# Expert weights two tiles to a transfer, in rows of 8 KB, with buffers given out in rows of two

## The chip, the cores and the metric

The program runs on one core of a Trainium2 chip. The metric is the device time of one execution in microseconds (us); the time before is the median of three runs. The profile is that of one execution of the same program.

## The reference

Two layers of a decoder work on 256 tokens of width 1024, all in float32. Each layer computes

```
h = rms(x); p = h @ W_in                       # q 8x64, k 2x64, v 2x64, u 512
x = x + W_o [ rms(window_attention(q,k,v)) ; rms(ssm(u)) ]
x = x + ffn(rms(x))
```

The feed-forward part of layer 0 is a dense SwiGLU, `(silu(h Wg) * (h Wu)) Wd` with an inner width of 3584. That of layer 1 is a mixture: a router picks two of eight such SwiGLU experts for every token, and the two results are added with softmax gates. The eight experts' weights are 352 MB of the 420 MB that the program reads from HBM (High Bandwidth Memory, the chip's main memory).

## The kernel before

**How the work is staged.** First the mixer of layer 0 (projection, attention, state-space model, output projection; until about 205 us), then the dense feed-forward part in 7 chunks of 512 inner columns (until about 450 us, with the mixer of layer 1 worked into its end), then the routing (480 to 494 us), then the experts (until 1407 us), then the output. The experts are sorted by how many tokens they got and taken in the order `TURNS = (0, 4, 1, 5, 2, 6, 3, 7)`: places 0 to 3 are heavy (room for 128 tokens), places 4 to 7 are light (room for 64). So a heavy expert and a light one alternate, each in 7 chunks.

**A chunk of an expert.** It takes 12 weight tiles, each of 128 partitions x 1024 float32 (512 KB, one DMA each, 4 KB to a partition): 4 of the gate matrix, 4 of the up matrix, 4 of the down matrix. To multiply float32 at one pass per column, `split` makes two fp32r tiles of a loaded tile `w`: ScalarE copies it, rounded, to `wh`, VectorE subtracts to get `wl = w - wh`. A heavy expert then has three matmuls for each of the two halves of a tile (`wh,xh`, `wl,xh`, `wh,xl`), 72 in a chunk. A light expert holds the high and the low half of its 64 tokens side by side in one operand (`lx`), has two matmuls per half tile, and folds the halves together afterwards (`join`). Of its 12 tiles one (`ENTIRE`) is not split but multiplied in plain float32. After gate and up come silu (ScalarE), a product on VectorE in `glu_up` or `light_up`, four transposes, a split of the result, and the down matmuls, which are written out one chunk late behind the next chunk's gate and up.

**Buffers.** All wide tiles come out of one pool `m` of `NM = 44` buffers of 4 KB a partition: `w`, `wh`, `wl`, the gathered tokens, the results. Narrower ones come out of a pool `h` of 8.

**What sets the order.** `Plan` records every operation, and `order` plays them through with modelled costs (`cost`, `lag`, `between`, `rate`) and priorities: the longest path to the end plus a hand-given number per stage (`BONUS`, 35 entries). The order in which operations start in this play is the order of the program, engine by engine; the play also counts free buffers, holds some back (`keep`, from `KR` and `LEAN`) and limits the split tiles alive. DMAs are all issued by SP (SyncE) in the order of the loads; a DMA whose buffer is not free yet waits on SP's queue, and everything behind it waits too. The loads of the first expert (place 0) name their address outright; later ones take the expert's number from a register, which is known once the routing is done.

**Names in the profile.** All operations are emitted by one line, L445 (`emit`), so rows are told apart by tile names: `w`, `wh`, `wl`, `xh`, `xl` (heavy tokens), `lx` (light tokens), `sg` (the product of gate and up), `ht`, `hth`, `htl` (its transposes), `yh`, `yl` (the result), `X` (the running x), `rw` (the router's weights).

The lines that load a tile and split it:

```python
    def load(self, src, whole=False):
        w = self.M("w")
        self.plan.keep = self.kr
        ...
        self.nc.sync.dma_start(w, src)
        ...
        return (w, None) if whole else self.split(w)
```

Of the kernel before, what the change touches and what calls it, by code (L numbers as in the profile page):

```python
# [26 lines left out]
ROOM = 64  # L27
# [40 lines left out]
class Buf:  # L68
    def __init__(self, plan, kind, shape, dtype, name):
        self.kind, self.shape, self.dtype, self.name = kind, shape, dtype, name  # L70
        self.real = None
        self.log = []
        self.users = 0
        self.live = False
        self.cols = int(np.prod(shape[1:]))
# [53 lines left out]

class Late:  # L130
# [19 lines left out]
class Plan:  # L150
    between, rate = 0.0027, 360e3

    def __init__(self):
        Plan.between, Plan.rate = 0.0027, 360e3
# [17 lines left out]
    def add(self, eng, method, a, k):  # L172
        i = len(self.ops)
        out = [x for x in (a[0], k.get("accum_out")) if isinstance(x, View)]
        src = [x for x in (*a[1:], *(v for n, v in k.items() if n != "accum_out")) if isinstance(x, View)]
# [35 lines left out]
    def cost(eng, method, a, k):  # L211
# [3 lines left out]
        if eng == "DMA":  # L215
            return int(np.prod(a[0].shape)) * 4 / Plan.rate + 0.01
# [7 lines left out]
        if eng == "ACT":  # L224
            return 0.05 + n * 0.000876 + (0.06 if any(isinstance(v, View) for v in k.values()) else 0)
        if eng == "POOL":
            return max(0.35, 0.05 + n * 0.0006)
        if method in ("tensor_scalar", "tensor_copy"):
# [6 lines left out]
    @staticmethod  # L235
    def lag(e, f):

        return 0.0 if e == f == "PE" else LAT[e] + (0.13 if f == "PE" and e != "DMA" else 0.0)

    def order(self, slots):  # L240
# [13 lines left out]
        for i, o in enumerate(ops):  # L254
            prio[i] += self.bonus.get(o["tag"], 0.0)
        free = dict(slots)
        engines = ["PE", "DVE", "ACT", "POOL", "DMA"]
# [48 lines left out]
        while done < n:  # L306
# [14 lines left out]
            while freed and freed[0][0] <= t:  # L321
                _, kd, name = heapq.heappop(freed)
                free[kd] += 1
                raw -= name == "w"
# [5 lines left out]
            while avail[e]:  # L330
# [7 lines left out]
                if (due or not o["turn"] or split < o["most"] and o["turn"] == turn) and all(  # L338
                        free[kd] - c >= (o["keep"] if kd == "m" and not due and (raw > 1 or not o["dma"]) else 0)
                        for kd, c in need.items()) and (due or not need or safe(x[1])):  # L340
# [35 lines left out]
            o = ops[i]  # L376
            for b in o["bufs"]:
# [33 lines left out]
            for b in o["bufs"]:  # L411
                users[id(b)] = users.get(id(b), 0) + 1
                if users[id(b)] == b.users and b.kind in free:
                    heapq.heappush(freed, (end, b.kind, b.name))
# [13 lines left out]
    def emit(self, nc, make, order):  # L428
# [11 lines left out]
        for i in order:  # L440
            o = self.ops[i]
            if o["method"] == "registers":
                o["a"][2](real(o["a"][1]))
                continue
            getattr(engines[o["eng"]], o["method"])(*map(real, o["a"]), **{n: real(v) for n, v in o["k"].items()})  # L445


class Kernel:
# [3 lines left out]
    BONUS = {'qkv1': -5, 'att0': 43, 'att0s': 29, 'prep0': 5, 'us1': -15, 'xt0': 8, 'ssm1y': -83, 'ssm0g': 60, 'u0': -47, 'wo01': 87, 'qkv0': 2, 'hn': -49, 'route': -33, 'wo011': 54, 'att1s': -26, 'prepo1': -82, 'moe': -5, 'route1': -2, 'att0v': 10, 'rs': -22, 'wo11': 8, 'ssm0': 3, 'route0': 42, 'ssm1': 5, 'wo010': -5, 'att1v': 40, 'xt1': 12, 'us0': 5, 'gates': 5, 'prep1': 15, 'ssm1g': 20, 'att1': 2, 'wo10': 2, 'wo110': -2, 'u1': -2}  # L452
# [3 lines left out]
    hold, spare = [], 0  # L456
# [8 lines left out]
    def __init__(self, tc, ctx, aps):  # L465
# [4 lines left out]
            ("k", 1, {}), ("m", self.NM, {}), ("h", self.NH, {}), ("s", 2, {}), ("ps", 8, {"space": PSUM}))}  # L470
# [5 lines left out]
    def make(self, b):  # L476
        return self.new(b.kind, b.shape, b.dtype, b.name)
# [34 lines left out]
    def load(self, src, whole=False):  # L512
        w = self.M("w")
# [4 lines left out]
        self.nc.sync.dma_start(w, src)  # L518
# [76 lines left out]
    def inv_rms_turned(self, x, n, name):  # L595
# [8 lines left out]
        return self.inv_root(bank[:, 0:2], n, name)  # L604

# [542 lines left out]
    def glu_up(self, src, of, blocks, rs):  # L1148
# [42 lines left out]
    def route(self, rs, gain):  # L1191
# [3 lines left out]
        rw = self.rw  # L1195
        tt(rw.rearrange("p (k e) -> p k e", k=8), self.rw.rearrange("p (k e) -> p k e", k=8),
# [117 lines left out]
    def gather(self, es, hn):  # L1314
# [13 lines left out]
        for b in range(2 * n):  # L1328
            bank = self.bank()
            for i in range(4 // n):  # L1330
                k = 4 // n * b + i
                for j, (x, t) in enumerate(src):
                    p = PP[:, m * t:m * t + m]
                    nc.tensor.matmul(bank[:, m * i:m * i + m], x[:, 128 * k:128 * k + 128], p if hn else p.bitcast(F32),
                                     start=j == 0, stop=j == len(src) - 1)
            for i in range(4 // n):
# [3 lines left out]
                g = self.mg[:, k:k + 1]  # L1340
# [389 lines left out]
```

## Time and profile before

| what | value |
|---|---|
| median of 3 runs | 1419.53 us (1416.21 to 1420.21) |
| the profiled execution | 1417.69 us, of it 1415.9 us from the first to the last instruction |
| TensorE busy, matmuls | 1374.0 us (97%), 6550 matmuls |
| VectorE busy | 1204.1 us (85%) |
| ScalarE busy | 998.9 us (71%) |
| moved by DMA | 422.57 MB, 298 GB/s over the span |
| loads of expert weights | 672 of 512 KB |
| granted TensorE clock, mean | 0.993 |

Matmuls are pipelined and each row's duration overlaps the next, so a TensorE that is "busy" is not necessarily at its pace; the distance between the starts of two matmuls tells more. The DMA share is the mean busy share of the core's 16 DMA engines in a stretch; it can come out a little over 1.

### The profile page before, as it was taken

What the parts mean: (1) busy time and instruction counts of PE and PEld (TensorE: products, weight loads), DVE (VectorE), ACT (ScalarE), POOL (GpSimd) and SP (SyncE); (2) the same over time, 40 slices, a digit from 0 to 9 for tenths busy, and PEclk for the clock granted to TensorE, in tenths of its full rate; (3) what the DMA queues carried; (4) which work ended last, traced back from release to release, by engine and by line L of the source; (5) the groups of instructions that cost most, each with busy time, mean ns of one, the idle gap of its engine ahead of it and who ended that gap; (6) DMA issues with size and microseconds to landing.
All of it is one profiled execution on the core that took longest, in us unless ns stands there. A gap on an engine that the chain in (4) does not pass through costs nothing.

```text
span 1415.9 us, 20663 instructions
## 1 busy us (share of the span) xinstructions
PE 1374.0 (97%) x6550; PEld 1073.1 (76%) x6550; DVE 1204.1 (85%) x1642; ACT 998.9 (71%) x1314; POOL 25.5 (2%) x44
## 2 busy tenths in 40 slices
PE   7999999999999999999999999999999999999996
PEld 4888888888888878877678876778887667887654
DVE  8889985554685699999989889989989999998987
ACT  5486754444527387799787788878779778787775
POOL 3000110000000000000000000000000000000000
PEclk9999999999999999999999999999999999999999
DMA  6357155555546759689999999999999999999993
GB/s 220 101 172 252 46 161 177 192 193 162 168 141 240 296 192 360 251 334 397 359 375 371 394 388 406 395 352 370 390 387 393 395 408 372 385 381 400 409 408 146
DMA packets 116899, 422.57 MB, mean 298 GB/s; under 512 B 13360, under 2 KB 13872, under 8 KB 116784
## 3 DMA queue, kind: packets, MB, share of 16 engines
q1 hardware_dynamic: 116784, 421.20, 79.5%
q8 instruction: 53, 0.87, 0.2%
q14 instruction: 62, 0.51, 0.1%
HBM read 420.10 MB, written 1.05 MB: 297 GB/s over the span
## 4 chain that ended last, share of the span: by engine, by line
PE 85%; DVE 6%; DMA 3%; issue 3%; ACT 2%; SPq 0%; DVEq 0%; ACTq 0%
PE bank L445 85%; DVE wl L445 4%; DMA w<-in_moe_dram 3%; ACT wh L445 2%; DMA w<-in_win_u_dram 1%; DVE X L445 1%; ACT st L445 0%; SPq L445 0%; DVE ht L445 0%; DVE htl L445 0%; ACT xh L445 0%; DVE psm L445 0%; DVE xl L445 0%; ACT L445 0%; DVE yl L445 0%
## 5 line engine op out<-in xcount | busy, mean ns | idle before, releaser
L445 DVE TENSOR_TENSOR wl<-w,wh 128x1024 fp32r<-128x1024 f32 x758 | 882.7, 1215 | 86.8 <-ACT wh L445 54.2
L445 ACT ACTIVATE wh<-w 128x1024 fp32r<-128x1024 f32 x758 | 749.3, 1052 | 80.3 <-DMA w<-in_dense_dram 29.5
L445 PE MATMUL bank<-wh,xh 128*128 128x512 f32 x448 | 174.8, 396 | 2.8 <-DVE ht L445 1.9
L445 PE MATMUL bank<-wl,xh 128*128 128x512 f32 x448 | 171.7, 394 | 0.8 <-DVE wl L445 0.8
L445 PE MATMUL bank<-wh,xl 128*128 128x512 f32 x448 | 171.5, 393 | 0.1
L445 PE MATMUL bank<-wl,lx 128*128 128x512 f32 x392 | 159.0, 407 | 8.3 <-DVE wl L445 7.9
L445 PE MATMUL bank<-wh,lx 128*128 128x512 f32 x392 | 152.4, 398 | 8.6 <-DVE ht L445 4.7
L445 PE MATMUL bank<-wh,hth 128*128 128x512 f32 x336 | 115.5, 399 | 0.0
L445 PE MATMUL bank<-wh,htl 128*128 128x512 f32 x336 | 114.5, 399 | 0.0
L445 PE MATMUL bank<-wl,hth 128*128 128x512 f32 x336 | 114.4, 396 | 0.0
L445 PEld LDWEIGHTS bank<-wl,lx 128*128 128x128 f32 x392 | 74.5, 190 | 41.8 <-DVE wl L445 26.6
L445 PEld LDWEIGHTS bank<-wh,xh 128*128 128x128 f32 x448 | 84.0, 188 | 22.0 <-ACT wh L445 2.9
L445 PEld LDWEIGHTS bank<-wl,xh 128*128 128x128 f32 x448 | 84.4, 188 | 20.8 <-DVE wl L445 3.2
L445 PEld LDWEIGHTS bank<-wh,xl 128*128 128x128 f32 x448 | 84.0, 189 | 17.7 <-DVE xl L445 0.5
L445 PEld LDWEIGHTS bank<-wh,lx 128*128 128x128 f32 x392 | 74.3, 190 | 26.3 <-ACT wh L445 6.5
L445 PE MATMUL bank<-wh,hh 128*128 128x512 f32 (+1 forms) x288 | 91.5, 385 | 0.4
L445 PE MATMUL bank<-wl,hh 128*128 128x512 f32 (+1 forms) x288 | 90.1, 381 | 0.0
L445 PE MATMUL bank<-wh,hl 128*128 128x512 f32 (+1 forms) x288 | 90.0, 380 | 0.0
L445 PE MATMUL bank<-wh,ht 128*128 128x512 f32 x224 | 89.0, 431 | 0.6 <-ACT wh L445 0.6
L445 PE MATMUL bank<-wl,ht 128*128 128x512 f32 x224 | 84.6, 406 | 2.0 <-DVE wl L445 2.0
L445 PEld LDWEIGHTS bank<-wh,htl 128*128 128x128 f32 x336 | 62.8, 188 | 14.4 <-issue 1.2
L445 PEld LDWEIGHTS bank<-wh,hth 128*128 128x128 f32 x336 | 62.5, 188 | 14.0 <-issue 0.5
(308 smaller groups left out, 1732.1 us busy)
## 6 DMA issues: line engine op xcount, KB each, us to landing
w<-in_moe_dram SPq DMA_DIRECT2D x672, 512.0 KB, 6.3
w<-in_dense_dram SPq DMA_DIRECT2D x84, 512.0 KB, 4.3
w<-in_wo_dram SPq DMA_DIRECT2D x16, 512.0 KB, 4.4
w<-in_win_u_dram SPq DMA_DIRECT2D x8, 512.0 KB, 5.1
w<-in_win_q_dram SPq DMA_DIRECT2D x8, 512.0 KB, 7.6
w<-in_win_kv_dram SPq DMA_DIRECT2D x4, 512.0 KB, 3.6
w<-in_wglu_dram SPq DMA_DIRECT2D x4, 512.0 KB, 3.6
X<-in_x_dram SPq DMA_DIRECT2D x2, 512.0 KB, 4.2
```

What stands on the lines that cost most here:

```text
L445: getattr(engines[o["eng"]], o["method"])(*map(real, o["a"]), **{n: real(v) for n, v in o["k"].items()})
```

## The change

**Two tiles to a transfer.** For all experts but the first (`j > 0`), tiles 2q and 2q+1 of a chunk come in one DMA of 1 MB. The 256 rows of 4 KB are read as 128 rows of 8 KB: partition p of tile j holds rows 2p and 2p+1, so the contraction index of the gate, up and down matrices is permuted. The other operands are brought into the same order: the tokens by `wide` copies in `split_rows` and a `block(k)` in the gathers, the hidden values by `wide` products, and the gain by four small DMAs that write a permuted copy of it behind the router's weights.

**Buffers in rows of two.** The pool `m` becomes 22 rows of two buffers. The plan itself now chooses the row: a pair of weight tiles takes an idle row, a single buffer the free half of a row in use with the same type, or else half of an idle row; of several, the one idle longest. A transfer that is not the next in order must leave another row idle.

**Products without the scale.** The factor `rs` on the up half is left out of the product and put on the result in `scatter` instead. With `wide`, one VectorE operation of 512 columns with a scalar from memory becomes two `tensor_tensor` of 256 columns; for the first expert it becomes one `tensor_tensor` of 512.

**Costs and priorities.** The modelled gap between matmuls is 0.0135 us in the whole program (before: 0.0027 until the experts), the lag to TensorE 0.03 in place of 0.13, a scan costs twice as much per element, and a transfer of two tiles is reckoned at 1.025 of the rate. `BONUS` has 106 entries, 68 of them for a stage on one engine (`'rs/DVE': -60`).

The core of the diff (the new `BONUS` table, the same edits inside `overflow`, which runs only when an expert's room is exceeded, and the plan's bookkeeping are left out):

```diff
...
+def block(k):
+
+    return 4 * (k // 2 % 2) + 2 * (k % 2) + k // 4
...
-    between, rate = 0.0027, 360e3
+    between, rate = 0.0135, 360e3
...
-        return 0.0 if e == f == "PE" else LAT[e] + (0.13 if f == "PE" and e != "DMA" else 0.0)
+        return 0.0 if e == f == "PE" else LAT[e] + (0.03 if f == "PE" and e != "DMA" else 0.0)
...
+        rows = [Row() for _ in range(slots["m"] // 2)]
+
+        def seat(bufs):
+
+            at = [(max(r.idle), n) for n, r in enumerate(rows) if None not in r.idle]
+            if len(bufs) == 1:
+                at = [(r.idle[q], n, q) for n, r in enumerate(rows) for q in range(2)
+                      if r.idle[1 - q] is None and r.idle[q] is not None and r.dtype == bufs[0].dtype] or at
+            if not at:
+                return False
+            _, n, *q = min(at)
+            return n, q[0] if q else 0
+
+        def fits(bufs):
+
+            return None in rows[seat(bufs)[0]].idle or sum(None not in r.idle for r in rows) > 1
...
     def load(self, src, whole=False):
-        w = self.M("w")
+        if isinstance(src, Half) and src.half:
+            return (self.other, None) if whole else self.split(self.other)
+        w, also = self.M("w"), {}
+        if isinstance(src, Half):
+            src, self.other = src.pair, self.M("w")
+            also = {"also": self.other}
...
+    def wide(dst, src):
+
+        dst = [x.rearrange("t (r c j p) -> t r j c p", r=2, c=2, p=64) for x in dst]
+        src = [x.rearrange("t (j c p r) -> t r j c p", r=2, c=2, p=64) for x in src]
+        return [[x[:, r] for x in (*dst, *src)] for r in range(2)]
...
-            self.stt(h, ub[t], rs[:, t:t + 1], h, OP.mult, OP.mult)
+            if wide:
+                g, h = h, self.H("hs")
+                for o, u, v in self.wide([h], [ub[t], g]):
+                    self.tt(o, u, v, OP.mult)
+            elif blocks == 1:
+                self.tt(h, ub[t], h, OP.mult)
+            else:
+                self.stt(h, ub[t], rs[:, t:t + 1], h, OP.mult, OP.mult)
...
-                    w = [Late(lambda j=j, i=i, q=q: e[bass.ds(self.regs[j], 1), i, q].rearrange("o p n -> (o p) n")) for q in range(12)]
+                    w = [Late(lambda j=j, i=i, q=q: e[bass.ds(self.regs[j], 1), i, 2 * q:2 * q + 2].rearrange("o j (p r) n -> (o j p) (r n)", r=2)) for q in range(6)]
+                    w = [Half(w[q // 2], q % 2) for q in range(12)]
...
-            self.act(hi, self.X[t], AF.Copy)
-            self.tt(lo, self.X[t], hi.bitcast(F32), OP.subtract)
+            for h, x in self.wide([hi], [self.X[t]]):
+                self.act(h, x, AF.Copy)
+            for q, h, x in self.wide([lo, hi.bitcast(F32)], [self.X[t]]):
+                self.tt(q, x, h, OP.subtract)
...
-            self.act(y[0][:, c], acc[h], AF.Copy)
-            self.tt(y[1][:, c], acc[h], y[0][:, c].bitcast(F32), OP.subtract)
+            self.act(y[0][:, c], acc[h], AF.Copy, scale=rs)
+            self.stt(y[1][:, c], acc[h], rs, y[0][:, c].bitcast(F32), OP.mult, OP.subtract)
...
+        for s in range(2):
+            for r in range(2):
+                nc.sync.dma_start(self.rw[64 * s:64 * s + 64, 64:].rearrange("p (q r c) -> p r q c", q=2, r=2)[:, r],
+                                  a["prm"][1][:, 90:98].rearrange("(p r) (q s c) -> r s p q c", r=2, q=2, s=2)[r, s])
...
```

## Rows read from the trace of the kernel before

**Rows 1.** The page: busy time, share of the span, instructions, of two engines.

```profile
PE 1374.0 (97%) x6550; PEld 1073.1 (76%) x6550; DVE 1204.1 (85%) x1642; ACT 998.9 (71%) x1314; POOL 25.5 (2%) x44
```

**Rows 2.** Busy time of each engine by stretch, granted clock, DMA share, GB/s.

```profile
core 0: us, PE busy (x) PEld busy (x) DVE busy (x) ACT busy (x) POOL busy (x), PEclk, DMA share, GB/s
0.00:21.00 21.00, 13.35 (x38) 7.37 (x38) 14.05 (x73) 12.90 (x30) 11.11 (x19) 1.00 0.83 315
21.00:205.00 184.00, 183.76 (x1054) 146.81 (x1055) 164.94 (x386) 119.63 (x209) 11.45 (x19) 1.00 0.43 139
...
480.00:500.00 20.00, 17.93 (x110) 15.99 (x108) 13.95 (x80) 8.65 (x17) 0.00 (x0) 0.83 0.48 181
...
580.00:610.00 30.00, 30.00 (x157) 24.01 (x156) 27.15 (x39) 22.34 (x29) 0.00 (x0) 1.00 0.52 172
610.00:690.00 80.00, 77.79 (x328) 56.63 (x327) 79.08 (x80) 70.58 (x85) 0.00 (x0) 1.00 1.02 400
...
830.00:930.00 100.00, 97.06 (x425) 72.65 (x424) 95.75 (x101) 87.02 (x108) 0.00 (x0) 1.00 1.02 401
...
1060.00:1180.00 120.00, 113.63 (x463) 81.75 (x463) 113.63 (x116) 98.17 (x118) 0.00 (x0) 0.99 1.02 400
1180.00:1280.00 100.00, 99.83 (x451) 81.48 (x450) 93.27 (x89) 76.28 (x86) 0.00 (x0) 1.00 0.99 376
1280.00:1385.00 105.00, 98.88 (x395) 67.36 (x394) 94.93 (x95) 83.51 (x100) 0.00 (x0) 1.00 1.02 407
1385.00:1416.00 31.00, 20.72 (x77) 12.65 (x76) 21.20 (x24) 14.88 (x19) 0.00 (x0) 0.94 0.29 110
```

**Rows 3.** Stretches again, matmuls that read `lx` alone (light experts).

```profile
611.00:736.00 125.00, 66.98 (x224) 0.99 0.99 382
...
836.00:955.00 119.00, 64.99 (x224) 0.99 0.99 388
...
1057.00:1186.00 129.00, 66.53 (x224) 0.99 1.02 399
...
1284.00:1407.00 123.00, 67.37 (x224) 1.00 0.89 353
```

**Rows 4.** The chain that ended last, pieces: start us, us, what.

```profile
675.70 6.74 DMA w<-in_moe_dram
...
941.25 153.08 PE bank L445 x675
...
1187.78 130.76 PE bank L445 x581
...
1344.61 5.43 DMA w<-in_moe_dram
```

**Rows 5.** Waits of SP's DMA queue: us in total, times, longest us.

```profile
SPq L445 <- PE bank L445: 698.5, 461, 28.2
```

**Rows 6.** DMA queues, 1300 to 1380 us: packets, MB, share of 16 engines; issues to landing.

```profile
q1 hardware_dynamic: 8955, 32.60, 102.2%
...
w<-in_moe_dram SPq DMA_DIRECT2D x62, 512.0 KB, 7.4
```

**Rows 7.** DMA queues, 1400 to 1416 us: the output, written in rows of 2 KB.

```profile
q1 hardware_dynamic: 576, 1.05, 17.7%
```

**Rows 8.** DMA queues in half a microsecond, 1298.2 to 1298.7 us.

```profile
q1 hardware_dynamic: 53, 0.20, 98.3%
q14 instruction: 1, 0.01, 4.0%
```

**Rows 9.** Groups by form, 500 to 1410 us: busy us, mean ns, idle before.

```profile
L445 DVE SCALAR_TENSOR_TENSOR sg<-bank,rse,sg 128x512 f32<-128x512 f32 x28 | 20.9, 747 | 9.7 <-PE bank L445 9.7
...
L445 DVE TENSOR_TENSOR ht<-bank,ht 128x256 fp32r<-128x256 f32 x28 | 11.4, 409 | 0.2
```

**Rows 10.** Timeline of VectorE: start us, us, what.

```profile
1204.14 11.43 DVE L445 TENSOR_TENSOR wl<-w,wh 128x1024 fp32r<-128x1024 f32 x10
```

**Rows 11.** Timeline of SP's queue around 76 us.

```profile
76.73 0.43 SPq L445 DMA_DIRECT2D rw<-in_router_dram  x1
```

More of the change, by code (lines that the diff above doesn't have):

```diff
@@ L127, in get, with __init__ @@
         return ap
+class Row:
+    def __init__(self, dtype=None, idle=(0.0, 0.0)):
+        self.dtype, self.idle = dtype, list(idle)
+        self.real = None
+class Half:
+    def __init__(self, pair, half):
+        self.pair, self.half = pair, half
+def block(k):
+    return 4 * (k // 2 % 2) + 2 * (k % 2) + k // 4
 class Late:
@@ L254, in order, with settle @@
         for i, o in enumerate(ops):
-            prio[i] += self.bonus.get(o["tag"], 0.0)
+            prio[i] += self.bonus.get(o["tag"], 0.0) + self.bonus.get(f"{o['tag']}/{o['eng']}", 0.0)
         free = dict(slots)
+        rows = [Row() for _ in range(slots["m"] // 2)]
[10 more added lines that the diff above has]
+            return None in rows[seat(bufs)[0]].idle or sum(None not in r.idle for r in rows) > 1
+        def settle(bufs):
+            n, q = seat(bufs)
+            if None not in rows[n].idle:
+                rows[n] = Row(bufs[0].dtype, rows[n].idle)
+            for b in bufs:
+                b.slot, rows[n].idle[q] = (rows[n], q), None
+                q += 1
         engines = ["PE", "DVE", "ACT", "POOL", "DMA"]
@@ L321, in order @@
             while freed and freed[0][0] <= t:
-                _, kd, name = heapq.heappop(freed)
+                when, kd, name, _, s = heapq.heappop(freed)
                 free[kd] += 1
+                if kd == "m":
+                    s[0].idle[s[1]] = when
                 raw -= name == "w"
@@ L376, in order @@
             o = ops[i]
+            new = [b for b in o["bufs"] if not b.live and b.kind == "m"]
+            if new:
+                settle(new)
             for b in o["bufs"]:
@@ L455 @@
     LEAN = (14, 7)
-    hold, spare = [], 0
+    hold, spare, other = [], 0, None
     FIRST = (3, 0, 1, 2)
@@ L476, in make @@
     def make(self, b):
+        if b.kind == "m":
+            row, q = b.slot
+            if row.real is None:
+                row.real = self.new("m", [128, 2048], row.dtype, "row")
+            return row.real[:, 1024 * q:1024 * q + 1024]
         return self.new(b.kind, b.shape, b.dtype, b.name)
@@ L1424, in light_up @@
         h = self.H("sg")[0:ROOM]
-        self.act(h, g[0], AF.Silu, scale=rs)
-        self.stt(h, g[1], rs, h, OP.mult, OP.mult)
+        self.act(h, g[0], AF.Silu, scale=rs[0:ROOM])
+        u, h = h, self.H("hs")[0:ROOM]
+        for o, x, v in self.wide([h], [g[1], u]):
+            self.tt(o, x, v, OP.mult)
         bank = self.bank()
@@ L1503, in split_rows, with scatter @@
         return hn
-    def scatter(self, place, j, PT, acc):
+    def scatter(self, place, j, PT, acc, rs):
         y = []
```

79 lines of the change are left out of this document (46 added, 33 removed).

## The prediction

> **What bounds the kernel now.** I read the page first. TensorE counts as busy for 97% of the span [rows 1], but matmuls overlap, so that share says little. The busy times by stretch come next, because the stages have different limits [rows 2]. Until 480 us the DMA share is about a half and no load is late, so a faster transfer is worth nothing there. From 610 us on the program alternates between two kinds of stretch. In one of a heavy expert (1180 to 1280 us) TensorE starts 451 matmuls in 100 us; the chain of waits runs through TensorE alone for 153.08 us with 675 matmuls, 0.227 us each [rows 4]. That is TensorE's pace, and DMA, at a share of 0.99 and 376 GB/s, has nothing to give. The matmuls on `lx` show where the light experts lie [rows 3]; inside those, in four stretches of together 405 us (610 to 690, 830 to 930, 1060 to 1180, 1280 to 1385), the DMA share is 1.02 at 400 to 407 GB/s [rows 2]. Fewer matmuls start there: 395 in 105 us, which at the heavy pace of 4.51 a microsecond would take 88 us. Here the chain has waits for weights in it [rows 4]. So the light experts are limited by transfers, and only their 405 us can answer to a faster one. What those stretches lack at the heavy pace is 80 − 328/4.51 = 7, 100 − 425/4.51 = 6, 17 and 17 us, together 47 us: no cure of the transfers can bring more.
>
> Two other things are to be seen. SP's queue waits 698.5 us for TensorE to give a buffer free [rows 5]: transfers are issued as buffers allow, and a 512 KB tile lands 7.4 us after its issue [rows 6]. As one takes 524288 B / 408 GB/s = 1.285 us, there are 5.8 tiles in flight. And VectorE is busy for 79.08 of 80 us in the first light stretch, but for 94.93 of 105 in the last [rows 2]: in the first it would be the next limit at once.
>
> **Rows of 8 KB.** From 1300 to 1380 us the queue has 32.60 MB in packets of 4 KB, which makes 7959, and about 1000 tiny ones; 102.2% of 16 engines x 80 us is 1308 us, or 164.4 ns per 4 KB with its share of the tiny ones [rows 6]. The trace has no weight load in 8 KB rows. The lower bound is no gain: 8 KB takes 328.8 ns. For the upper I take the output, in 2 KB rows: 17.7% of 16 x 16 us is 45.3 us for 512 packets, 88.5 ns each [rows 7]. Two of these are 177.0 ns, so a packet saved at that size saves 12.6 ns; one saved in 328.8 ns would be 3.8%. The nearest row is an instruction fetch, one packet of 8 KB amid the loads: 4.0% of 8 us is 320 ns [rows 8], 2.4% under 328.8 (1.2 to 3.6% by the rounding). I take 2.4%, as it is a read of the right size at the right time.
>
> The Trainium skill, page "DMA: Bandwidth & Descriptors", section "Why small descriptors are slow (HBM only)", gives a fixed overhead of about 3 cycles a packet beside 32 bytes a cycle. By an estimate from that, 8 KB in one packet takes 259 cycles and in two 262, 1.1% less, and the term below would be about 4 us instead of 8.7. The trace's 2.4% is above it, but by little more than its rounding.
>
> On the three later light stretches 2.4% of 325 us is 7.8 us; in the first VectorE has 0.9 us left. Together −8.7 us; the bounds are 0 and 0.9 + 3.8% of 325 = −13.3.
>
> **Pairs.** A loaded row is free only when both halves are split, and a transfer waits until a whole row is idle and another remains. Until now each freed buffer started a transfer. This makes the stock of tiles with which a light stretch begins smaller, by nothing (the splits `wh` and `wl` are pairs too and die together) up to two tiles. A tile is 1.285 us, there are four such stretches: 0 to +10.3 us. I take half a tile each, +2.6, since a half waits for its partner for one split, 1.14 us [rows 10], about as long as a tile takes to arrive. The issues are halved on SP's queue; that costs nothing, as it is the buffers that it waits for [rows 5]. At the end two tiles land together where one did, and the second is split 1.14 us later: +1.1. This is on the path, since 1385 to 1416 us is nothing but tail.
>
> **Products.** A 512-column product with a scalar takes 747 ns; two 256-column operations like `ht`'s take 818 [rows 9], 71 ns more in 49 chunks, 3.5 us of VectorE. Where VectorE has idle time (5 to 10% in the later light stretches) that costs nothing; in the first one it is on the path, 5 chunks, +0.4; with the cover gone everywhere it would be 3.5. The scale moved to `scatter` adds a scalar operand to the 16 splits of the result, at most 70 ns each, and the `wide` copies of `split_rows` are a few more operations during the first expert, where TensorE has its pace. They count as nothing, at most 1 us each. The four gain loads stand on SP's queue before the dense weights: 4 x 0.43 us of issue [rows 11], in a part with a DMA share of 0.43 [rows 2]. That cover makes them free; without it they cost 1.7 us.
>
> **Order and priorities.** What the new play does can't be read from a trace of the old. The modelled spacing of matmuls becomes 512/2400 + 0.0135 = 0.227 us, the very figure of the chain [rows 4]; before, it was short by 0.011 until the experts. TensorE's idle time ahead of the experts is small: 21 − 13.35 = 7.7 us at the start, 20 − 17.93 = 2.1 us in the routing [rows 2]. With better priorities at most these 9.8 us come back, and as many could be lost. I take −6, since the model now agrees with the rows on which it rests.
>
> **Sum.** −8.7 + 2.6 + 1.1 + 0.4 − 6 = −10.6 us. The profiled execution took 1417.7 us, 1.8 under the median of the runs and inside their spread, so I leave it as the base: 1407 us. By the terms' bounds the sum lies between −23.1 (−13.3 − 9.8) and +26.4 (10.3 + 1.1 + 3.5 + 3.7 + 9.8, less than nothing from the rate; 3.7 for the hidden edits), bounds that won't all meet.
>
> **Rivals.**
> The order gives more. The plan now seats a transfer in the row idle longest, so SP may wait less for TensorE than 698.5 us [rows 5], and stretches such as 580 to 610 us, where the DMA share falls to 0.52 although light work follows [rows 2], may hand a larger stock to the light experts. If half of the 47 us that the light stretches lack comes back, that is −24 in place of −8.7 and +2.6: 1417.7 − 24 − 4.5 = 1389 us. Against it: heavy stretches have been at a share of 0.99, and pairs lessen the stock.
>
> The rate doesn't change. If bytes and not packets set the 408 GB/s, the −8.7 is gone and 1416 us remain, no change. The 88.5 ns of a 2 KB packet, more than half of 164.4, speak against it, but that is the write side; for it speaks how near 320 and 328.8 are. The Trainium skill has a rule this way: the same page, section "Where 436 GB/s comes from", says that loads from HBM are bound by the memory at some 358 GB/s per core, whatever the descriptor. The trace disagrees, as it moves 408 GB/s, so that limit at least isn't the one in force here.
>
> Pairs starve the queue (slower). The place is the light stretches, the mechanism `fits` and a half-used row: with one transfer of 1 MB in flight and the next not issued, the engines run dry between two. The DMA share there would fall from 1.02, to 0.96 say; then 405 us become 430, and 1417.7 + 25 + 1.5 − 6 = 1438 us. For it speaks that SP's queue waits for buffers already [rows 5]; against it that 5.8 tiles, nearly three rows, are in flight. It decides once the share falls under about 1.00, where 8 us are lost.
>
> **How the numbers follow.** Chances: the forecast 0.50, the order giving more 0.18, the rate unchanged 0.15, pairs starving the queue 0.17. The likeliest case gives 1407 us, by itself 1398 to 1416. Within 0.3% of 1419.5, 1415.3 to 1423.8, is what a measurement of this kernel can't tell from no change. Faster: 0.46 of the forecast's 0.50, 0.18, and 0.06 of the unchanged rate (when the priorities bring more than 6), 0.70. The same: 0.04, 0.09 and 0.02, 0.15. Slower: 0.15, the rest of the starved queue. The range reaches to both neighbours, 1387 to 1430, and leaves out some 0.05 below and 0.12 above.
>
> **What the profile will show.** Rate: loads of 1 MB in packets of 8 KB at about 320 ns, and 410 to 418 GB/s in the light stretches at a share of 1.00 or more; 400 to 408 would be the unchanged rate. Pairs: a share in those stretches under 1.00 shows the starved queue. Light stretches shorter by about 2 to 3 us each, heavy ones with 4.5 matmuls a microsecond as before. Order: the first heavy matmul after the routing, now near 494 us, comes up to 6 us sooner. VectorE at 100% in light stretches with DMA under 1.00 would mean that VectorE has become the limit. What makes the forecast wrong: packets still of 4 KB, a share that falls, or a routing that ends later.

## Result and the profile after

The changed kernel takes 1441.49 us (median of 4 runs, 1439.73 to 1442.46), the kernel before 1419.87 beside it: ratio 1.0155, interval 1.0133 to 1.0177. It is slower, where I forecast 1407, and above the end of my range, 1430. The profiled execution took 1440.65 us, 1438.9 of it span.

Where the 23 us lie is read from marks in both timelines: the last write of `X` in a stage, the first write of `PPl` (start of the gather for light experts), the last `X`. The experts' own lengths are the distances between the first silus of one and the next.

| mark, us | before | after | difference grows by |
|---|---|---|---|
| mixer 0 ends | 131.6 | 140.0 | 8.4 |
| dense part ends | 374.1 | 381.0 | −1.5 |
| mixer 1 ends | 480.8 | 498.0 | 10.3 |
| light gather starts | 588.8 | 612.2 | 6.2 |
| last `X` | 1409.5 | 1432.4 | −0.5 |

So the whole loss is ahead of the light experts; from the gather on both need the same, 820.7 and 820.2 us. That equality is a gain and a loss that cancel, as e1 shows below. A mark carries some 4 us of its own: e4, which executes the same instructions as after up to the experts, has 136.7, 378.3, 496.6 and 610.7. By these marks the stages of before also end sooner than the "about 205" and "about 450" us that stand ahead of the prediction: mixer 0 at 131.6, the dense part at 374.1 us.

A part of the 6.2 us up to the gather is the clock. In the routing of after, TensorE was granted 0.71 of its clock over 20 us, in that of before 0.83 (480 to 500 us [rows 2]); in both it had stretches without work there. By an estimate from these two figures that is (0.29 − 0.17) x 20 = 2.4 us of TensorE's time.

```profile
500.00:520.00 20.00, 17.40 (x87) 15.62 (x87) 15.00 (x77) 8.52 (x16) 0.00 (x0) 0.71 0.59 200
```

The page of after, busy time by engine [rows 1]:

```profile
PE 1387.4 (96%) x6550; PEld 1071.3 (74%) x6550; DVE 1219.5 (85%) x1694; ACT 1014.3 (70%) x1316; POOL 25.3 (2%) x44
```

Its stretches: start, mixer 0, then a light, a heavy, and the three other light experts [rows 2, 3].

```profile
core 0: us, PE busy (x) PEld busy (x) DVE busy (x) ACT busy (x) POOL busy (x), PEclk, DMA share, GB/s
0.00:21.00 21.00, 12.25 (x32) 6.67 (x32) 13.15 (x50) 11.34 (x25) 11.11 (x19) 0.92 0.45 159
21.00:140.00 119.00, 114.89 (x732) 88.07 (x731) 106.94 (x252) 74.69 (x147) 1.38 (x6) 1.00 0.50 179
...
642.00:752.00 110.00, 106.90 (x467) 77.97 (x466) 106.23 (x122) 92.47 (x118) 0.00 (x0) 1.00 1.00 412
752.00:868.00 116.00, 115.92 (x513) 91.92 (x512) 106.63 (x106) 91.78 (x101) 0.00 (x0) 1.00 0.96 377
868.00:981.00 113.00, 108.13 (x466) 78.39 (x466) 109.53 (x128) 93.24 (x116) 0.00 (x0) 1.00 0.97 398
...
1096.00:1204.00 108.00, 102.29 (x410) 73.42 (x409) 102.35 (x108) 91.15 (x110) 0.00 (x0) 0.97 0.98 399
...
1321.00:1409.00 88.00, 85.23 (x336) 58.73 (x335) 84.81 (x93) 74.36 (x89) 0.00 (x0) 0.98 0.98 407
```

The DMA queue of after in a light stretch, 1330 to 1380 us, with the issues to landing [rows 6, 8]:

```profile
q1 hardware_dynamic: 2862, 20.84, 100.6%
...
row<-in_moe_dram SPq DMA_DIRECT2D x23, 1024.0 KB, 9.1
```

20.84 MB in packets of 8 KB make 2544, the rest are tiny; 100.6% of 16 x 50 us is 805 us, or 316 ns each with its share of the tiny ones. Two of 4 KB took 328.8 by the same reckoning: the packets of 8 KB are 3.8% cheaper, the upper bound of my estimate, and the queue moves 418 GB/s. The tiny packets go by the transfer, 16 to each in both traces (996 for 32.60 MB in tiles of 512 KB, 318 for 20.84 MB in pairs of 1 MB), so a part of the 3.8%, which no run separates, is that there are half as many of them. The rate came, and bought nothing.

SP's queue at the start of after, and what it waited for in the first 20 us; it issues in order, so everything below a row waits for that row:

```profile
2.62 0.91 SPq L504 DMA_DIRECT2D row<-in_win_u_dram  x2
3.57 0.43 SPq L504 DMA_DIRECT2D row<-in_bc_dram  x1
18.09 0.80 SPq L504 DMA_DIRECT2D row<-in_win_u_dram  x2
18.93 0.43 SPq L504 DMA_DIRECT2D row<-in_win_q_dram  x1
...
SPq L504 <- PE bank L504: 9.5, 1, 9.5
SPq L504 <- DMA row<-in_win_u_dram: 4.5, 1, 4.5
```

The same load in before:

```profile
4.10 0.95 SPq L445 DMA_DIRECT2D w<-in_win_u_dram  x2
```

The third tile of the first weight matrix is issued at 18.09 us; before, at 4.10. `seat` has put it into the half of a row that an earlier tile of this matrix has just left in the play, because a half of a row in use comes ahead of idle rows; in the run that tile isn't done with yet, and SP waits for its landing and then for TensorE. So the first 21 us move 159 GB/s, where it was 315 [rows 2].

### The profile page after: what moved, and what is told of

Its sections match the earlier page's. It is cut to its first block, busy times and chain, and to the rows that moved or that the text cites. A ratio compares the mean times of both kernels' runs of the same rounds, so it can differ in the third digit from the quotient of the medians.

```text
span 1438.9 us, 19497 instructions
## 1 busy us (share of the span) xinstructions
PE 1387.4 (96%) x6550; PEld 1071.3 (74%) x6550; DVE 1219.5 (85%) x1694; ACT 1014.3 (70%) x1316; POOL 25.3 (2%) x44
## 5 line engine op out<-in xcount | busy, mean ns | idle before, releaser
L504 PE MATMUL bank<-row 128*128 128x512 f32 (+5 forms) x4192 | 995.9, 381 | 33.1 <-DVE row L504 13.2
L504 DVE TENSOR_TENSOR row<-row 128x1024 fp32r<-128x1024 f32 (+4 forms) x826 | 929.8, 1168 | 114.7 <-ACT row L504 59.1
L504 ACT ACTIVATE row<-row 128x1024 fp32r<-128x1024 f32 (+2 forms) x810 | 794.0, 1023 | 243.1 <-PE bank L504 186.2
L504 PEld LDWEIGHTS bank<-row 128*128 128x128 f32 (+2 forms) x4192 | 701.1, 182 | 237.6 <-DVE row L504 39.3
L504 PE MATMUL bank<-row,hth 128*128 128x512 f32 x672 | 207.9, 396 | 0.1
L504 PEld LDWEIGHTS bank<-row,hth 128*128 128x128 f32 x672 | 124.9, 188 | 26.6 <-ACT hth L504 1.0
L504 PE MATMUL bank<-row,ht 128*128 128x512 f32 x448 | 131.1, 409 | 1.2 <-DVE ht L504 0.9
L504 PE MATMUL bank<-row,htl 128*128 128x512 f32 x336 | 113.4, 393 | 0.4 <-DVE htl L504 0.4
L504 PEld LDWEIGHTS bank<-row,ht 128*128 128x128 f32 x448 | 82.6, 188 | 27.4 <-issue 5.4
L504 PEld LDWEIGHTS bank<-row,htl 128*128 128x128 f32 x336 | 62.9, 188 | 14.0 <-DVE htl L504 1.1
L504 ACT ACTIVATE hth<-bank 128x512 fp32r<-128x512 f32 x42 | 24.5, 588 | 28.4 <-PE bank L504 28.2
```

## Experiments

One table for all runs, each against the kernel before on the same chip. Marks are those of each run's profile; they carry some 4 us of their own (e14 and e15 execute the same instructions up to the experts, and lie 4.3 apart at the end of mixer 0). Lengths are steadier: from the gather to the last `X`, two runs that differ only in the size of the rows agree within 0.5 us.

| run | median us | ratio [95%] | mixer 0 | dense | mixer 1 | gather | last X |
|---|---|---|---|---|---|---|---|
| e1 new play, single buffers | 1437.03 | 1.0135 [1.0115, 1.0155] | 135.9 | 382.6 | 502.6 | 612.4 | 1427.2 |
| e2 after, old table | 1444.62 | 1.0185 [1.0166, 1.0204] | 150.7 | 385.8 | 493.0 | 604.9 | 1435.9 |
| e3 after, seat idle longest | 1430.47 | 1.0077 [1.0055, 1.0100] | 137.1 | 377.7 | 493.9 | 605.0 | 1423.2 |
| e4 after, pairs in 4 KB rows | 1440.31 | 1.0162 [1.0139, 1.0184] | 136.7 | 378.3 | 496.6 | 610.7 | 1430.9 |
| e5 table alone | 1425.30 | 1.0049 [1.0033, 1.0066] | 134.2 | 373.6 | 490.3 | 599.0 | 1415.5 |
| e6 lag and element costs alone | 1440.43 | 1.0142 [1.0117, 1.0167] | 136.3 | 384.6 | 502.9 | 612.9 | 1430.4 |
| e7 after, two whole tiles | 1448.63 | 1.0221 [1.0200, 1.0243] | 136.5 | 377.7 | 496.2 | 610.4 | 1435.3 |
| e8 e7 in 4 KB rows | 1445.99 | 1.0202 [1.0178, 1.0225] | 137.7 | 379.1 | 497.5 | 611.9 | 1436.3 |
| e9 after, three tiles high only | 1438.76 | 1.0153 [1.0124, 1.0181] | 138.6 | 380.0 | 496.9 | 609.1 | 1423.7 |
| e10 e9 in 4 KB rows | 1433.66 | 1.0102 [1.0082, 1.0121] | 139.4 | 380.5 | 500.4 | 614.7 | 1429.5 |
| e11 lag alone | 1417.99 | 0.9989 [0.9977, 1.0001] | 133.1 | 376.7 | 482.5 | 593.9 | 1409.5 |
| e12 element costs alone | 1434.01 | 1.0101 [1.0074, 1.0127] | 141.1 | 384.7 | 494.3 | 603.8 | 1423.5 |
| e13 pairs, old play | 1431.06 | 1.0068 [1.0050, 1.0087] | 136.0 | 381.2 | 488.9 | 597.8 | 1424.0 |
| e14 e13, play at 450 GB/s | 1426.52 | 1.0045 [1.0030, 1.0059] | 136.1 | 381.2 | 489.0 | 600.0 | 1420.0 |
| e15 e14 in 4 KB rows | 1425.67 | 1.0041 [1.0023, 1.0058] | 131.8 | 377.0 | 484.7 | 595.6 | 1415.5 |
| e16 singles, play at 450 GB/s | 1414.14 | 0.9951 [0.9934, 0.9969] | 134.9 | 378.6 | 484.5 | 596.7 | 1407.8 |
| e17 e14, seat idle longest | 1419.38 | 1.0009 [0.9995, 1.0023] | 135.0 | 379.1 | 486.8 | 597.5 | 1411.9 |
| e18 gap alone | 1426.72 | 1.0059 [1.0038, 1.0079] | 146.7 | 378.5 | 491.9 | 601.0 | 1422.0 |

### The play: priorities and costs (e1, e2, e5, e6, e11, e12, e18)

e1 is the kernel before with the new `BONUS` and two changed costs. The gap is set once more in `Plan.__init__`, where it stayed 0.0027, so e1 and e6 test lag and element costs (ScalarE's scaled copies and sums, the scan), not the gap.

```diff
...
-            return 0.05 + n * 0.000876 + (0.06 if any(isinstance(v, View) for v in k.values()) else 0)
+            more = 0.1 if any(isinstance(v, View) for v in k.values()) and a[1].buf.kind != "ps" else 0
+            return 0.05 + n * 0.000876 + more + (0.09 if "accum_out" in k else 0)
...
+        if method == "tensor_tensor_scan":
+            return 0.07 + n * 0.00204
...
-        return 0.0 if e == f == "PE" else LAT[e] + (0.13 if f == "PE" and e != "DMA" else 0.0)
+        return 0.0 if e == f == "PE" else LAT[e] + (0.03 if f == "PE" and e != "DMA" else 0.0)
...
-            prio[i] += self.bonus.get(o["tag"], 0.0)
+            prio[i] += self.bonus.get(o["tag"], 0.0) + self.bonus.get(f"{o['tag']}/{o['eng']}", 0.0)
...
```

> The kernel before with the new modelled costs and the new priorities alone: single buffers, one tile to a transfer. Three theories of the 22 us. Seats: single loads now go into the half of a row that was freed last, so they wait on SP's queue for its last reader; then this kernel has none of that and stays near 1420 us (1414 to 1425). Priorities: the new order itself is longer ahead of the experts; then most of the 22 us are here, 1436 to 1445 us, with the first heavy matmul after the routing some 20 us late. Pairs: the experts lose their gain to transfers of two tiles; that says nothing of the part ahead of them, so about 1420 here.

Without any pair, row or 8 KB packet the new play (but for its gap) costs 19 us, and the light gather starts at 612.4, where after has 612.2. Mixer 1 alone is 120.0 us long against 106.7. The experts are shorter than before, 814.8 us from the gather to the last `X` against 820.7. e2 is the reverse, after with the old table:

> The changed kernel with the table of priorities of the kernel before; rows, pairs and the new modelled costs stay. Seats: no cure, 1436 to 1446 us, and the third weight load of the program is still issued at about 18 us. Priorities: the part ahead of the experts comes back to its old length (first expert some 20 us sooner), 1415 to 1424 us.

Mixer 1 falls back to 107.2 us, but mixer 0 ends at 150.7: the old table does not suit the new costs and seats either (e18 below, the old table with the new gap alone, has 146.7). e5 keeps the new table of e1 and takes back both costs; e6 keeps the costs and takes back the table.

> The kernel before with the new priorities table alone (and its entries for single engines), the modelled costs as before. Before took about 1419, with table and costs both new 1437 with mixer 1 120 us long (before 107). If the table does the harm: 1433 to 1440, mixer 1 118 to 122 us long. If the new costs do it and the table only goes with them: 1417 to 1424, mixer 1 107 to 110.

> The kernel before with the new modelled costs alone, the priorities table as before. If the table does the harm: 1415 to 1424, mixer 1 105 to 110 us. If the costs do it: 1430 or more, mixer 1 115 us or longer. A third way is that the two only do harm together: then this run and the one with the table alone are both near 1420.

It is the costs that do the harm, 21 us, with mixer 1 118.3 us long. The table alone costs 6, between my two ranges: its mixer 1 is long too (116.7), but its dense part ends early. e11 and e12 divide the costs, e18 sets only the gap, in both places:

```diff
-        Plan.between, Plan.rate = 0.0027, 360e3
+        Plan.between, Plan.rate = 0.0135, 360e3
```

> The kernel before, with one modelled cost changed: the lag from another engine to TensorE 0.03 in place of 0.13 us. With the new costs of lag, copies and scans all together the time was 1440, mixer 1 about 12 us longer. If the short lag does the harm: 1432 or more, mixer 1 115 us or longer. If the costs of copies and scans do it: 1416 to 1424.

> The kernel before, with the new modelled costs of ScalarE's scaled copies and sums and of the scan alone, the lag as before. If these do the harm: 1432 or more, mixer 1 115 us or longer. If the short lag does it: 1416 to 1424. If the two share it: both near 1430.

> The kernel before with the modelled gap between matmuls 0.0135 in place of 0.0027 us ahead of the experts, table and other costs as before. It agrees with the measured spacing, so my prediction reckoned with a gain, up to 6 us: 1412 to 1419. If, as with the other costs, a changed cost only upsets a table of priorities made for the old ones: 1425 to 1440, mixer 1 110 us or longer.

The last writes of `X` in mixer 1, from the lists of tile `X` of e6 and then of e11 (first and last start at the end of the times):

```profile
L448 DVE SCALAR_TENSOR_TENSOR X<-bank,so_y,X x4: 750/752/753, 496.2 to 502.1; 128x512 f32<-128x512 f32 x4
```

```profile
L445 DVE SCALAR_TENSOR_TENSOR X<-bank,so_y,X x4: 751/752/753, 475.8 to 481.7; 128x512 f32<-128x512 f32 x4
```

The same four operations of the same length, 20 us apart: the instructions are the old ones, only their order differs. The lag is harmless, the element costs cost 14 us (with mixer 1 only 109.6 us long), and the gap, the one cost that agrees with the measured spacing of 0.227 us [rows 4], costs 8, with mixer 0 ending 15 us late. A changed cost gave a worse order in three runs of four (e6, e12, e18, not e11).

### Seats (e3)

In after, a single weight tile now takes the half idle longest, of rows in use and idle rows alike:

```diff
-                at = [(r.idle[q], n, q) for n, r in enumerate(rows) for q in range(2)
-                      if r.idle[1 - q] is None and r.idle[q] is not None and r.dtype == bufs[0].dtype] or at
+                half = [(r.idle[q], n, q) for n, r in enumerate(rows) for q in range(2)
+                        if r.idle[1 - q] is None and r.idle[q] is not None and r.dtype == bufs[0].dtype]
+                at = half + [x + (0,) for x in at] if bufs[0].name == 'w' else half or at
```

> The changed kernel with one choice in seat altered: a single weight tile takes the half that has been idle longest, be it in a row in use or in an idle row, and not first a half of a row in use. Seats: the third weight load is issued at about 4 us and not at 18, the mixers get back their 8 to 18 us, 1422 to 1433 us. Priorities: the loads come sooner, but the mixers are as long as before, 1437 to 1443 us.

```profile
0.00:21.00 21.00, 13.94 (x40) 7.48 (x40) 13.91 (x71) 12.19 (x28) 11.13 (x19) 1.00 0.90 340
```

The first 21 us are back at 340 GB/s and the run is 11 us faster than after, in the range for "seats". But the mixers don't get their 8 to 18 us back: mixer 0 ends 2.9 us sooner than in after, less than a mark carries, and no sooner than in e4 (136.7), which has the wait at the start; mixer 1 is still 116.2 us long. Of the rest, 4.3 us come ahead of the light gather and 2.0 in the experts. So the wait at the start can't be seen at the end of mixer 0, and why the other seats save 11 us in all is not shown; a different seat makes another order all along.

### Rows of 8 KB (e4, e7 to e10, e14, e15)

e4 keeps pairs, seats and order of after, and only splits each transfer:

```diff
-                nc.sync.dma_start(x.buf.slot[0].real, real(o["a"][1]))
+                both = real(o["a"][1]).rearrange("p (r n) -> r p n", r=2)
+                nc.sync.dma_start(real(x), both[0])
+                nc.sync.dma_start(real(y), both[1])
```

> The changed kernel with each pair fetched by two transfers in rows of 4 KB (every second row each) into the same row of buffers; order, seats and products are the same. If the faster packet is worth what the prediction said, about 9 us, this takes 1450 us (1446 to 1454), with 405 to 410 GB/s in the light stretches. If pairs ate it, because the engines run dry between transfers of 1 MB, the time is 1438 to 1443 us, and two issues instead of one fill the gaps.

Two stretches, of after and then of e4; the first lies in a light expert, the second begins with some 8 us of a heavy one:

```profile
645.00:705.00 60.00, 57.05 (x241) 41.31 (x241) 58.98 (x63) 52.72 (x65) 0.00 (x0) 1.00 1.01 422
860.00:920.00 60.00, 56.81 (x231) 39.87 (x229) 58.38 (x62) 51.75 (x63) 0.00 (x0) 1.00 1.00 411
```

```profile
645.00:705.00 60.00, 57.10 (x242) 41.43 (x241) 58.99 (x63) 52.78 (x65) 0.00 (x0) 1.00 1.03 410
860.00:920.00 60.00, 56.50 (x230) 39.87 (x230) 58.38 (x64) 51.46 (x63) 0.00 (x0) 1.00 1.02 400
```

In e4, 12 and 11 GB/s less go through the queue, and VectorE does the same work in the same time. The 1440.3 us lie in the range that I gave to pairs, but the engines don't run dry between transfers of 1 MB: the share of after is 1.01 and 1.00 here. The lengths of the experts are the same to 0.1 us: 106.6, 109.6, 115.5, 113.5, 114.9, 108.1, 116.7 in e4 against 106.7, 109.6, 115.6, 113.5, 114.8, 108.0, 116.7. How this goes with a DMA share over 1 and with transfers in the chain is seen in the last light expert: the chain's shares by line, 1321 to 1400 us, of after and then of e4.

```profile
by line: PE bank L504 86.4%; DVE row L504 5.5%; ACT row L504 4.5%; issue 2.2%; ACT low L504 0.8%; ACT sg L504 0.7%; ACT ht L504 0.3%; DVEq L504 0.1%
```

```profile
by line: PE bank L506 73.6%; DMA row<-in_moe_dram 10.2%; DVE row L506 7.6%; ACT row L506 5.1%; issue 2.3%; ACT low L506 0.8%; ACT sg L506 0.7%; ACT ht L506 0.3%; DVEq L506 0.1%
```

With 4 KB rows 10.2% of the chain are transfers, with 8 KB none, and the expert takes 111.9 and 111.8 us: so the transfer can have been last only by a hair, and with it gone another chain of the same length stands there.

VectorE, busy for 58.98 of 60 us, was the next suspect. e7 multiplies a second tile of a light chunk whole in float32, so that VectorE need not split it; e8 is e7 in 4 KB rows.

```diff
-ENTIRE = (7,)
+ENTIRE = (7, 9)
```

> The changed kernel, with a second tile of a light chunk multiplied whole in float32 and not split: VectorE loses a split of 1.14 us in each of 28 light chunks, TensorE gets slower float32 passes in its place. If VectorE and the order bind the light stretches and transfers don't: each light expert is 3 to 7 us shorter, 1415 to 1430 in all. If transfers bind them: the light experts stay as long, 1438 to 1444. If TensorE has no time to give there: longer, 1445 to 1465.

> The run before it, but each pair by two transfers in rows of 4 KB. With one whole tile a chunk the size of the rows made no difference (1440.3 against 1441.5). If VectorE hid the gain of the faster transfers, and now has room: slower than the run before it by 3 to 8 us. If the order or the buffers bind and not transfers: the same within 2 us.

The same stretch of after and then of e7:

```profile
640.00:720.00 80.00, 76.90 (x323) 55.18 (x322) 78.98 (x85) 69.49 (x86) 0.00 (x0) 1.00 1.01 419
```

```profile
640.00:720.00 80.00, 80.00 (x321) 55.67 (x318) 71.44 (x78) 66.95 (x81) 0.00 (x0) 1.00 1.01 421
```

VectorE falls from 99% to 89% and TensorE rises from 96% to 100%; of the light experts two gain 1.2 and 4.3 us and one loses 4.1, the first heavy one between them loses 4.3, and the run loses. Row sizes again make no difference: the lengths of e7 and e8 agree within 0.3 us. So e9 cuts both: tiles 1, 5 and 9 of a light chunk are multiplied by their high part alone (the low part's product is left out), the bytes stay.

```diff
+HIGH = (1, 5, 9)
...
-        lo = self.M("wl", F32R)
+        lo = self.M("wl", F32R) if low else None
...
+        if not low:
+            return hi,
...
```

> The changed kernel, with tiles 1, 5 and 9 of every light chunk multiplied by their high part alone: the low part's subtraction (VectorE, 3 x 1.14 us a chunk) and its two matmuls a tile (TensorE, 3 x 0.45 us a chunk) are left out, and so is that part of the product. The bytes loaded are the same. If VectorE and TensorE set the light experts' pace: these shrink from 108 to 114 us towards the 105 us that 44 MB take at 420 GB/s, 15 to 30 us in all, 1411 to 1427. If transfers set it: the light experts stay within 2 us each, 1434 to 1442.

> The run before it, but each pair by two transfers in rows of 4 KB. If with the engines' work cut the transfers have become the limit of the light experts, rows of 8 KB are worth 44 MB x (1/405 - 1/420 GB/s) = 3.9 us for each, 8 to 16 us in all: this run is that much slower than the run before it. If transfers are still not the limit: the same within 2 us.

The second light expert of e9, then of e10, and the chain of e9 through one chunk (1374 to 1392 us):

```profile
862.00:974.00 112.00, 103.25 (x426) 70.35 (x425) 88.41 (x104) 96.08 (x116) 0.00 (x0) 1.00 1.00 409
```

```profile
868.00:980.00 112.00, 103.20 (x426) 70.32 (x425) 88.39 (x104) 96.03 (x116) 0.00 (x0) 1.00 1.03 406
```

```profile
by line: PE bank L505 55.8%; DVE row L505 26.9%; ACT row L505 11.8%; issue 8.3%; DVE hs L505 1.5%; DVEq L505 0.2%; ACT low L505 0.1%
```

VectorE is at 79%, TensorE at 92%, ScalarE, whose copies are all left in, at 86%, and the expert still takes 112.5 us (113.5 in after), in both row sizes; the other two light ones take 108.5 and 111.0 (109.6 and 108.0). By its number e9 hits what I wrote for "transfers set it" (its four runs spread from 1431.7 to 1443.7, and the profile is of the fastest), but e10 denies that: transfers 3% dearer change no length by more than 0.4 us. This piece of e9's chain holds no transfer. It goes from TensorE to ScalarE's copy to VectorE's split and back to TensorE: hand-offs in the written order, while each engine by itself has room. In e10, loads of expert weights make 10.5% of the chain over the whole span, in e9 they don't appear in it: as in e4, they can be last only by a hair. e13 (below) and e14 ask whether another order helps: the play reckons the experts' transfers at 390 GB/s, e14 at 450.

```diff
-        Plan.between, Plan.rate = 0.0135, 390e3
+        Plan.between, Plan.rate = 0.0135, 450e3
```

> The run before it, with the rate at which the play reckons the experts' transfers 450 in place of 390 GB/s. The engines follow the order that the play writes, and the play at 390 GB/s writes one for slow transfers. If that order sets the light experts' pace: they shrink from 108 to 114 us towards 105, in all 8 to 25 us less than the run before it. If something else does (work of VectorE, transfers): within 5 us of it, either way.

> The run before it, but each pair by two transfers in rows of 4 KB. If with the other order transfers limit the light experts, the rows of 8 KB are now worth 2 to 3 us an expert: this run is 6 to 15 us slower than the run before it. If not: the same within 2 us, the times of the experts equal.

> The kernel before with the short lag (alone 1418.0) and the play's rate of 450 in place of 390 GB/s: single buffers, rows of 4 KB. If the order written for 390 GB/s holds the light experts back: 1400 to 1412. If real transfers at 400 to 408 GB/s do: 1415 to 1425, a DMA share of 1.02 in the light stretches as before.

e14 is 4.5 us faster than e13, inside the 5 us that I had set for "something else". Light experts of 94.2, 106.0 and 111.3 us stand beside a first heavy one of 125.7, so the order moves time between experts more than it saves. In e15 every length agrees with e14 within 0.2 us, but for the last, 0.4. e16, single buffers with the same play, is the fastest of all, 0.5% under the kernel before and between the two ranges that I gave it.

### Pairs under the old play (e13, e17)

e13 has the change's pairs, seats and products; table, gap and element costs are those of before, and the lag is e11's. So e11 is its twin on single buffers.

> The changed kernel (pairs in rows of 8 KB, rows of two, products without the scale), with the table of priorities, the gap between matmuls and the costs of copies and scans as before. Only the short lag to TensorE is kept, which alone gave 1418.0. If the pairs bring in the experts what the prediction gave them: 1409 to 1414. If the pace of the experts is set by the order and not by transfers, and the seats cost some us ahead of them: 1419 to 1427. If the rows themselves do the harm: 1435 or more.

e13 is 13 us slower than e11, between my two ranges for harm. The gather starts 3.9 us later, and the first two experts take 225.1 us against 208.5; later ones give 5.5 back. The first light expert, of e13 and then of e11:

```profile
630.00:745.00 115.00, 109.90 (x455) 81.48 (x455) 103.35 (x118) 90.45 (x114) 0.00 (x0) 0.94 0.94 387
```

```profile
625.00:725.00 100.00, 100.00 (x443) 75.07 (x443) 98.88 (x107) 89.77 (x114) 0.00 (x0) 1.00 1.01 397
```

Here the DMA share does fall, to 0.94, and TensorE's granted clock too. Both come from one place in e13:

```profile
710.00:720.00 10.00, 6.39 (x30) 6.42 (x31) 9.02 (x14) 2.81 (x6) 0.00 (x0) 0.58 1.00 418
720.00:730.00 10.00, 10.00 (x36) 7.97 (x36) 6.83 (x11) 6.55 (x9) 0.00 (x0) 0.74 0.15 38
```

TensorE first waits 4.31 us for a product of VectorE (`hs`), ahead of which six splits of together 6.88 us were written, while the DMA share is 1.00. Then it was granted 0.50, the lower of its two levels (1.2 GHz), from 712 to 724 us; by an estimate from the two rows that is (0.42 + 0.26) x 10 = 6.8 us of its time. Only from 721 us on does the queue run empty, as SP waits up to 13.7 us for TensorE to give a buffer free. So the order comes first here, and the empty queue behind it. e17 gives e14 the seats of e3 ahead of the experts:

> The run with pairs and the play at 450 GB/s (1426.5), with one change: ahead of the experts a single weight tile takes the half idle longest, of rows in use and idle rows alike, so that its load waits for no tile that is still in use. On single buffers the same play gave 1414.1. If the seats make the rest of the loss: the third load is issued in the first 5 us, mixer 0 ends near 133 us, and 1415 to 1421 in all. If the loss is in the experts (a transfer needs a whole idle row): 1421 to 1427.

SP's queue of e17, to set beside that of after:

```profile
3.57 0.44 SPq L502 DMA_DIRECT2D row<-in_bc_dram  x1
4.06 0.95 SPq L502 DMA_DIRECT2D row<-in_win_u_dram  x2
```

1419.4 us is in the range for "seats", but not by that way: only 2.5 of the 7 us against e14 are there at the gather, the rest comes in the experts. With pairs this is the best run, level with the kernel before and 5 us behind e16.

## Why the prediction was wrong

**Order and priorities, −6: the step that failed, in sign and size.** I bounded it by TensorE's 9.8 us of idle time ahead of the experts [rows 2], to both sides. That bounds a gain. A loss has no such bound, as a worse order makes idle time that was not there. On single buffers (e1) the new play, even without its gap, costs 19 us of the 22, and delays the gather by 23.6 against 23.4 in after. At the last `X`, 17.7 of the 22.9 us are there in e1; the other 5.2 come with the pairs. That its gap agrees with the rows was no ground for a gain: alone (e18) it costs 8 us. Why one order is better than the next, I can't say; parts do not add up (lag −2, inside the noise; elements +14, the two together +21, with the new table +19).

**Rows of 8 KB, −8.7: the rate was right, its worth was nothing.** 316 ns a packet was forecast as 320. (320 is 2.7% under 328.8, and not 2.4%; the term would have been −9.7.) The failed step stands ahead of it: "the light experts are limited by transfers". I took a DMA share of 1.02 for a limit [rows 2], and two pieces of the chain for all four light experts [rows 4]. The chain's shares in the second and third light expert of before (844 to 954, 1068 to 1183 us) hold no transfer; in the first and the last (620 to 731, 1295 to 1400 us) transfers make 18.3% and 15.0% of it. What a faster packet is worth was measured on the orders of after, e7, e9 and e14, not on that of before:

```profile
by line: PE bank L445 76.5%; DVE wl L445 11.7%; issue 7.2%; DVE xl L445 1.0%; ACT wh L445 1.0%; DVE ht L445 0.8%; DVE yl L445 0.5%; DVE sg L445 0.5%; ACT xh L445 0.5%; DVE X L445 0.4%; DVEq L445 0.1%; ACT low L445 0.0%
```

```profile
by line: PE bank L445 74.4%; DVE wl L445 11.8%; issue 8.1%; ACT wh L445 3.5%; DVE ht L445 1.1%; DVE X L445 0.7%; ACT ht L445 0.3%; DVEq L445 0.2%; DVE sg L445 0.1%; ACT low L445 0.0%
```

And part of "the 47 us that these stretches lack" was no lack. TensorE's timeline of before, with the tile that a light chunk multiplies whole:

```profile
620.57 0.39 PE L445 MATMUL bank<-wl,lx 128*128 128x512 f32 x1
620.80 1.88 PE L445 MATMUL bank<-w,lx 128*128 128x512 f32 x4
622.52 0.49 PE L445 MATMUL bank<-K,sg 128*128 128x128 f32 x3
```

Its four records take 1.72 us to the next start (other such tiles 1.31), where four others take 0.91. Counting matmuls against the heavy pace turned 28 such tiles, 11 to 23 us, into idle time.

**The rate doesn't change**, my rival at 1416 us, named the wrong reason and the right worth. The Trainium skill, page "DMA: Bandwidth & Descriptors", section "Where 436 GB/s comes from", puts the fabric's ceiling at about 435 GB/s beside the 358 of the memory; this core moved 422 in a light stretch, so the trace is near the first and far above the second.

**Pairs, +2.6, and the rival that they starve the queue.** The right measure is a run with the same play on single buffers, from the gather to the last `X`: after takes 820.2 where e1 takes 814.8, e3 818.2, e13 826.2 where e11 takes 815.6, e14 820.0 and e17 814.4 where e16 takes 811.1. So the pairs, with the seats and products that come with them, cost the experts 3 to 11 us in every case. In after the new play hides this: it saves the experts 5.9 us (e1), and the pairs take 5.4 of them back. The term was too small, its bound of 10.3 about right. The share falls as the rival says, but not from 1.02 in before, which I had read from chosen stretches (over whole light experts before has 0.98, 0.99 and 1.02 in the first three): after has 1.00, 0.97 and 0.98 there, and e1, its twin on single buffers, 1.01, 1.00 and 1.02:

```profile
643.00:746.00 103.00, 101.86 (x449) 75.46 (x448) 102.00 (x110) 89.54 (x115) 0.00 (x0) 1.00 1.01 398
861.00:975.00 114.00, 109.91 (x469) 80.83 (x468) 109.39 (x120) 93.43 (x117) 0.00 (x0) 0.99 1.00 388
1086.00:1201.00 115.00, 109.25 (x440) 75.73 (x439) 109.25 (x111) 90.71 (x109) 0.00 (x0) 1.00 1.02 405
```

Whether a transfer that waits for a whole idle row makes the loss, or the order that the play writes for such rows, is not shown; in e13 it is an order first. That the rival's 1438 us stand so near the measured 1441 is luck: it expected 25 us in the experts, and the loss of after lies ahead of them. That the seats would make SP wait at the start I did not see; e3 and after's SP queue show it.

**Products and tail.** Products of 256 columns take 405 to 425 ns (409 forecast [rows 9]); no run singles them out. From the last `X` to the end of the span are 6.4 us before and 6.5 after.

**Bounds.** The terms of the upper bound add up to 28.4, not 26.4. The measured 24 us above the base lie inside both, but not term by term: the order alone went beyond its 9.8.

**What stays open.** The pace of the light experts: shown is that neither the packet's size, nor VectorE's load, nor TensorE's and VectorE's together set it in the order as written. ScalarE's load (86% in e9) was not cut by itself. That it is the hand-offs of that order is read from one chain and by exclusion; the one other order that I tried (450 GB/s) saved 4 us.

## What to carry to other kernels

A DMA share of 1 says that the queue always holds something, not that anyone waits for it: read the chain in each of the stretches that the gain is to come from, and try first, at no risk to the rest, whether a slower transfer hurts. Where a planner writes the order, a change of its costs or priorities is a change of the whole program, worth a run by itself ahead of any other edit. What a change does to a stage is read against a twin with the same order: beside before, the experts of after seemed to lose nothing. A rule that reuses a half-used buffer before an idle one puts a wait into an in-order queue, and everything behind it waits too.

## What was not expected of the hardware

Packets of 8 KB took 316 ns against 164.4 for 4 KB, each with its share of tiny ones, and 422 GB/s reached one core in a light stretch. A wait of 4.31 us in TensorE was followed by some 12 us at a granted clock of 0.50 (e13). Two programs with the same order and transfers 3% apart kept the lengths of seven experts to 0.1 us each, over 780 us. A pace in matmuls per microsecond misleads where float32 ones stand among them: up to 0.43 us a record here, against 0.227.
